# One block for the attention scores of a pair of heads, and unread products behind the last

## The chip, the core and the metric

The kernel runs on one core of one Trainium2 chip. Its engines work side by side, each through its own queue in order: TensorE (PE, with its weight loads as PEld), VectorE (DVE), ScalarE (ACT), GpSimd (POOL) and SyncE (SP, which here issues most of the copies between the chip's memory and the core). TensorE writes only into the eight accumulation banks (PSUM); DVE and ACT read them. The metric is the device time of one execution in microseconds.

## The reference

Two layers of a decoder trunk on 256 tokens of width 1024. The part that the change touches is the differential attention of 8 heads, each with two maps of head dimension 64:

```python
s = jnp.einsum('bqhmd,bkhmd->bhmqk', q_blk, k).astype(jnp.float32) * scale
...
s = jnp.where(mask, s, neg)
p = jax.nn.softmax(s, axis=-1)
a = p[:, :, 0] - lam * p[:, :, 1]
return jnp.einsum('bhqk,bkhe->bqhe', a.astype(v.dtype), v)
```

Around it stand projections, a spatial gating branch, two gated feed-forward networks per layer and layer norms:

```python
for l in range(DEPTH):
    h = _swiglu(x, ffn_w1[l, 0], ffn_w3[l, 0], ffn_w2[l, 0])
    x = _layernorm(ALPHA * x + 0.5 * h, ln_g[l, 0], ln_b[l, 0])
    h = _mixer(x, l, ...)
    x = _layernorm(ALPHA * x + h, ln_g[l, 1], ln_b[l, 1])
    h = _swiglu(x, ffn_w1[l, 1], ffn_w3[l, 1], ffn_w2[l, 1])
    x = _layernorm(ALPHA * x + 0.5 * h, ln_g[l, 2], ln_b[l, 2])
```

## The kernel before

Every large product is computed from operands split into a high and a low part in the type fp32r, which TensorE takes in one pass. The weights come as raw float32 (`raw`, 1 MB per load, four buffers, issued by SP at L153); ACT makes the high part (`whi`, L166) and DVE the low part (`wlo`, L168), each with eight buffers.

Two routines carry most of TensorE's work. `gemm_a2` (L210) takes the weights as the stationary operand. For each block of 128 output rows it issues eight products of 512 columns with the high weights (L220) and later eight products of 256 columns with the low ones (L227); a step for a pair of output blocks is thus 16 products of L220 and 16 of L227. ACT then reads one half of each bank (L228) and DVE adds the other (L230 or L232). `gemm_b` (L249) and `gemm_b2` (L269) take the tokens as the stationary operand, three products of 512 columns per block (L208); the very last call of `gemm_b` cuts its second tile of tokens into two parts of 256 columns, so that the last normalization can begin earlier.

The order of TensorE's instructions is the order in which the program text issues them. Smaller work is threaded in as "tasks": `beside(task, delay)` enters a generator, `beat(w)` moves a clock by the share of main work just issued (0.65 after eight products of L220, 0.35 after eight of L227, n/1024 after a row step of n columns), and a task whose time has come issues its next part at that point, until its next `yield d`, which sets it back by d. On ACT, DVE and POOL a scheduler orders the instructions by priority and by the hints in `behind(...)`.

The eight accumulation banks are four "main" ones for the large products and four "side" ones for everything threaded in. A new side bank waits until the readers of the tile that last had it are done.

The attention of a pair of heads `hp` goes as follows. `rope` projects q, then k, with `gemm_a2`; SP copies the halves of the result crosswise (`swap`, L545), POOL multiplies by the sines (L549), DVE by the cosines (L548), and DVE adds the two a little later (L553). The task `attend`, entered 3.9 after k, then does:

- scores of the second tile of tokens (`exps(1)`, L573): two side banks, one for each of the two maps, and four products of 256 columns, each over 64 partitions (the lower half for map 0, the upper for map 1), in plain float32, which is recorded as two passes a product;
- DVE adds the mask and takes the row maximum (L581), ACT the exponential and its sum (L583);
- 0.6 later the scores of the first tile (`exps(0)`): two more side banks, four products of 128 columns, and the same on DVE and ACT; then the division and the difference of the two maps on DVE (L599, L600, L592);
- 2.6 later six transposes (L607, L612) into two side banks, which ACT copies (L609, L614); 2.3 later the products with the values (L620, L622), read by ACT (L625, L630); then the norm on POOL (L633 and `rsqrt4`) and ACT (L639), transposes back (L644), and the split into `hb` by ACT and DVE (L649, L650).

Four such tasks per layer overlap with each other and with the projections that follow (the gates, `wa`).

Of the kernel before, what the change touches and what calls it, by code (L numbers as in the profile page):

```python
# [19 lines left out]
P = 128  # L20
# [9 lines left out]
HD = 64  # L30
# [20 lines left out]
def trunk(ctx, tc, x, xT, w13a, w13b, w2, wb, wqk, wa, wbr, wo, gateb, sgug, sgub, sguwT, sgubias, lam, diffg,  # L51
          lng, lnb, lngT, lnbT, cosT, sinT, out):
    nc = tc.nc
    V, A, G, PE = nc.vector, nc.scalar, nc.gpsimd, nc.tensor
# [15 lines left out]
    def name(s):  # L70
        serial[0] += 1
        return f"{s}_{serial[0]}"

    def bank():
        return psum.tile([P, 512], F32, tag="main", name=name("bank"))

    def side_bank():
        return psum.tile([P, 512], F32, tag="side", name=name("sbank"))

    def slots(s, n, dtype=F32):  # L80

        return [act.tile([P, 512], dtype, tag="slot", name=name(s)) for _ in range((n + 1) // 2)]
# [8 lines left out]
    def parts(f):  # L91
        return (lambda k: f(k)[:, :T]), (lambda k: f(k)[:, T:])
# [4 lines left out]
    def s512(s, n=4):  # L97
        return tmp.tile([P, 512], F32, tag="side", name=name(s), bufs=n)

    def sm(s, n, dtype=F32, bufs=2):  # L100
        return small.tile([P, n], dtype, tag=f"{s}{n}", name=name(s), bufs=bufs)
# [31 lines left out]
    def beside(task, delay):  # L133
        tasks.append([clock[0] + delay, task])
# [8 lines left out]
    def behind(ins):  # L143

        return tc.issue_after(ins) if ins is not None else nullcontext()
# [93 lines left out]
    def rows_b(ps, t, k0, piece, xh, xl, kts, c0=0, n=512):  # L239

        hi, lo = piece
        for j in range(2):
            k, o = k0 + j, j * 512 + c0
            wh, wl = (w[j][:, c0 : c0 + n] if isinstance(w, list) else w[:, o : o + n] for w in (hi, lo))
            three(ps[:, :n], xh(k)[:, t * P : (t + 1) * P], xl(k)[:, t * P : (t + 1) * P], wh, wl,
                  k == 0, k == kts - 1)
        beat(n / 1024)

    def gemm_b(src, kts, xh, xl, done, tail=4, last=()):  # L249

        blocks = [[(bank(), c, n) for c, n in (last if t else ()) or ((0, 512),)] for t in range(NT)]
        held = []
        for c in range(0, kts, 4):
            nk = min(4, kts - c)
            for i, piece in enumerate(stream(src[:, c * 512 : (c + nk) * 512], nk * 512)):
                k = c + 2 * i
                if k >= kts - tail:
                    held.append((k, piece))
                    continue
                for t in range(NT):  # L260
                    for ps, o, n in blocks[t]:
                        rows_b(ps, t, k, piece, xh, xl, kts, o, n)
        for t in range(NT):
            for ps, o, n in blocks[t]:
                for k, piece in held:
                    rows_b(ps, t, k, piece, xh, xl, kts, o, n)
                done(t, ps[:, :n], o, n)

    def gemm_b2(srcs, xh, xl, done, norm=None):  # L269

# [253 lines left out]
    def mixer(l, i, norm):  # L524
        xh, xl = parts(both)
# [33 lines left out]
        def attend(hp, qT, kT):  # L559
            mx, sums = sm("mx", 8), sm("sums", 8)  # L560
            c4 = sm("c", 4)
            rc = sm("rc", 4)

            def rows(z, m, j, o, n):
                return z[m * HD : (m + 1) * HD, j * T + o : j * T + o + n]

            def exps(t):

                nk = (t + 1) * P
                banks = [side_bank() for _ in range(2)]  # L570
                for j in range(2):
                    for m in range(2):
                        PE.matmul(banks[m][:, j * nk : (j + 1) * nk], rows(qT, m, j, t * P, P), rows(kT, m, j, 0, nk),  # L573
                                  start=True, stop=True)
                pp = []
                for m in range(2):
                    o = m * 4 + t * 2
                    p = s512("pp", 4)[:, : 2 * nk]
                    for j in range(2):
                        s, a = slice(j * nk, (j + 1) * nk), slice(o + j, o + j + 1)  # L580
                        V.tensor_tensor_reduce(out=p[:, s], in0=banks[m][:, s], in1=mask[:, T - nk :], scale=-1.0,  # L581
                                               scalar=BIG, op0=ALU.add, op1=ALU.min, accum_out=mx[:, a])
                        A.activation(p[:, s], p[:, s], AF.Exp, bias=mx[:, a], scale=-1.0, accum_out=sums[:, a])  # L583
                    pp.append(p)
                return pp

            def less(t, pp):

                nk = (t + 1) * P
                for j in range(2):  # L590
                    s = slice(j * nk, (j + 1) * nk)
                    V.scalar_tensor_tensor(out=pp[0][:, s], in0=pp[1][:, s], scalar=c4[:, t * 2 + j : t * 2 + j + 1],  # L592
                                            in1=pp[0][:, s], op0=ALU.mult, op1=ALU.add)
                return pp[0]

            second = exps(1)
            yield 0.6
            first = exps(0)
            V.reciprocal(out=rc, in_=sums[:, 4:])  # L599
            V.scalar_tensor_tensor(out=c4, in0=rc, scalar=neg_lam[l], in1=sums[:, :4], op0=ALU.mult, op1=ALU.mult)  # L600
            second, first = less(1, second), less(0, first)
            yield 2.6
            b = side_bank()
            for j in range(2):
                for c in range(2):
                    o = (j * 2 + c) * P
                    PE.transpose(b[:, o : o + P], second[:, o : o + P], ident)  # L607
            aT1 = slots("aT", 2)[0]
            A.activation(aT1, b, AF.Copy)  # L609
            b = side_bank()  # L610
            for j in range(2):
                PE.transpose(b[:, j * P : (j + 1) * P], first[:, j * P : (j + 1) * P], ident)  # L612
            aT0 = slots("aT", 2)[0][:, :T]
            A.activation(aT0, b[:, :T], AF.Copy)  # L614
            yield 2.3
            b = side_bank()
            for j in range(2):
                h = hp * 2 + j
                v = [val[c][:, h // 4, (h % 4) * P : (h % 4 + 1) * P] for c in range(2)]
                PE.matmul(b[:, j * P : (j + 1) * P], aT0[:, j * P : (j + 1) * P], v[0], start=True, stop=True)  # L620
                for c in range(2):
                    PE.matmul(b[:, T + j * P : T + (j + 1) * P], aT1[:, (j * 2 + c) * P : (j * 2 + c + 1) * P],  # L622
                               v[c], start=c == 0, stop=c == 1)
            on = slots("on", 2)[0]
            A.activation(on, b, AF.Copy)  # L625
            ss, s2 = sm("ss", 4), sm("s2", 4)
            A.activation(s2, sums[:, :4], AF.Square, scale=(2 * HD * EPS) ** 0.5)
            for q in range(4):
                s = slice(q * P, (q + 1) * P)
                A.activation(b[:, s], b[:, s], AF.Square, accum_out=ss[:, q : q + 1])  # L630
            yield 2
            with behind(turned_by[0]):
                G.tensor_tensor(out=ss, in0=s2, in1=ss, op=ALU.add)  # L633
            r = rsqrt4(ss, 1.0 / (2 * HD))
            yield 2
            for q in range(4):
                s = slice(q * P, (q + 1) * P)
                with behind(emptied[0]):
                    A.activation(on[:, s], on[:, s], AF.Copy, scale=r[:, q : q + 1])  # L639
            yield 0.9  # L640
            b = side_bank()
            for j in range(2):
                for t in range(NT):
                    PE.transpose(b[:, j * T + t * P : j * T + (t + 1) * P], on[:, (t * 2 + j) * P : (t * 2 + j + 1) * P],  # L644
                                  ident)
            dl = dgs[:, l : l + 1]
            for j in range(2):
                h, s = hb[hp * 2 + j], slice(j * T, (j + 1) * T)
                A.activation(h[:, :T], b[:, s], AF.Copy, scale=dl)  # L649
                V.scalar_tensor_tensor(out=h[:, T:], in0=b[:, s], scalar=dl, in1=h[:, :T].bitcast(F32),  # L650
                                        op0=ALU.mult, op1=ALU.subtract)

        for hp in range(HEADS // 2):
            qT = rope(wqk[l, hp, 0], HD ** -0.5)
            kT = rope(wqk[l, hp, 1], 1.0, hp == HEADS // 2 - 1)
            beside(attend(hp, qT, kT), 3.9)

        gates = []
        for br, sec in ((0, GA_), (1, GB_)):
# [17 lines left out]
        for t in range(NT):  # L677
            mv = sm("mv", 2)
            V.bn_aggr(out=mv, in_=vst[t])
            r = rsqrt(mv[:, 1:2], EPS)  # L680
# [152 lines left out]
```

## Time and profile before

| | |
|---|---|
| median of 3 runs | 1244.27 us (1244.17 to 1245.04) |
| profiled execution: its own time | 1244.4 us |
| its span, first to last instruction | 1242.7 us |
| mean granted clock of TensorE | 0.998 |
| DMA, mean over the span | 195 GB/s |

In a line of a group, the count of instructions follows the x, then come the total busy time in us, the mean of one in ns, and the idle time of its engine before them with what ended it. In a line of the timeline the start and the length in us come first; instructions of one kind in succession are put together (x8), from the start of the first to the end of the last. Products on TensorE overlap, so the distance between two starts says what a product costs, not its length.

### The profile page before, as it was taken

What the parts mean: (1) busy time and instruction counts of PE and PEld (TensorE: products, weight loads), DVE (VectorE), ACT (ScalarE), POOL (GpSimd) and SP (SyncE); (2) the same over time, 40 slices, a digit from 0 to 9 for tenths busy, and PEclk for the clock granted to TensorE, in tenths of its full rate; (3) what the DMA queues carried; (4) which work ended last, traced back from release to release, by engine and by line L of the source; (5) the groups of instructions that cost most, each with busy time, mean ns of one, the idle gap of its engine ahead of it and who ended that gap; (6) DMA issues with size and microseconds to landing.
All of it is one profiled execution on the core that took longest, in us unless ns stands there. A gap on an engine that the chain in (4) does not pass through costs nothing.

```text
span 1242.7 us, 17850 instructions
## 1 busy us (share of the span) xinstructions
PE 1233.4 (99%) x6695; PEld 1062.5 (86%) x6695; DVE 873.1 (70%) x1533; ACT 755.6 (61%) x1386; POOL 86.7 (7%) x182
## 2 busy tenths in 40 slices
PE   9999999999999999999999999999999999999997
PEld 8888888888888888888888888888888888888886
DVE  6766567876587977665677765679756879766753
ACT  6776446679665566664466664466785554766640
POOL 0100000244100000000000000002440000000000
PEclk9999999999999999999999999999999999999999
DMA  9755545654753645547545546556556456455540
GB/s 351 278 203 186 221 173 190 224 168 162 256 179 142 249 161 200 182 174 254 199 169 189 190 160 247 203 190 200 171 172 231 156 178 229 170 204 204 170 169 35
DMA packets 40679, 241.87 MB, mean 195 GB/s; under 512 B 5344, under 2 KB 6416, under 8 KB 14480
## 3 DMA queue, kind: packets, MB, share of 16 engines
q1 hardware_dynamic: 36624, 228.08, 51.7%
q0 software_dynamic: 3536, 12.13, 2.9%
q8 instruction: 52, 0.85, 0.3%
q10 hardware_dynamic: 432, 0.52, 0.1%
q14 instruction: 35, 0.29, 0.1%
HBM read 235.47 MB, written 1.05 MB: 190 GB/s over the span
## 4 chain that ended last, share of the span: by engine, by line
PE 99%; DVE 0%; DVEq 0%; issue 0%
PE bank L220 38%; PE bank L208 35%; PE bank L227 20%; PE bank L323 2%; PE sbank L573 1%; PE sbank L459 1%; PE sbank L622 1%; PE sbank L703 1%; PE sbank L335 0%; PE sbank L620 0%; PE sbank L644 0%; PE sbank L493 0%; PE sbank L607 0%; PE sbank L612 0%; DVE xtok L432 0%; DVE xtok L438 0%
## 5 line engine op out<-in xcount | busy, mean ns | idle before, releaser
L168 DVE TENSOR_TENSOR wlo<-raw,whi 128x1024 fp32r<-128x1024 f32 (+1 forms) x442 | 489.7, 1126 | 225.1 <-PE bank L227 129.9
L166 ACT ACTIVATE whi<-raw 128x1024 fp32r<-128x1024 f32 (+1 forms) x442 | 425.9, 978 | 278.8 <-PE bank L208 135.2
L220 PE MATMUL bank<-x,whi 128*128 128x512 f32 x1792 | 426.5, 392 | 0.0
L220 PEld LDWEIGHTS bank<-x,whi 128*128 128x128 f32 x1792 | 330.7, 188 | 69.0 <-issue 2.6
L227 PE MATMUL bank<-x,wlo 128*128 128x256 f32 x1792 | 229.9, 284 | 0.0
L227 PEld LDWEIGHTS bank<-x,wlo 128*128 128x128 f32 x1792 | 224.2, 191 | 4.7
L208 PE MATMUL bank<-whi,hhi 128*128 128x512 f32 (+1 forms) x374 | 141.2, 378 | 0.0
L208 PE MATMUL bank<-wlo,hhi 128*128 128x512 f32 (+1 forms) x374 | 141.0, 377 | 0.0
L208 PE MATMUL bank<-whi,hlo 128*128 128x512 f32 (+1 forms) x374 | 140.9, 377 | 0.0
L228 ACT ACTIVATE r<-bank 128x256 f32<-128x256 f32 x256 | 96.5, 380 | 66.2 <-PE bank L227 65.9
L208 PE MATMUL bank<-whi,x 128*128 128x512 f32 x328 | 106.6, 394 | 0.0
L208 PEld LDWEIGHTS bank<-whi,hlo 128*128 128x128 f32 x374 | 70.4, 188 | 13.1
L208 PEld LDWEIGHTS bank<-whi,hhi 128*128 128x128 f32 x374 | 70.4, 188 | 12.7
L208 PEld LDWEIGHTS bank<-wlo,hhi 128*128 128x128 f32 x374 | 70.4, 188 | 12.6
L208 PEld LDWEIGHTS bank<-whi,x 128*128 128x128 f32 x328 | 61.6, 188 | 12.6
L208 PE MATMUL bank<-wlo,x 128*128 128x512 f32 x164 | 64.0, 390 | 0.0
L465 ACT ACTIVATE xf<-sbank,ln_b,ln_g 128x128 f32<-128x128 f32 x80 | 30.1, 457 | 40.1 <-PE sbank L459 40.1
L230 DVE TENSOR_TENSOR silu<-bank,r 128x256 f32<-128x256 f32 x144 | 54.1, 417 | 0.2
L383 POOL DMA_DIRECT2D bc<-in_lng x6 | 3.2, 531 | 726.1 <-DVE bc L382 726.1
L409 DVE SCALAR_TENSOR_TENSOR xtok<-xtok,bank 128x512 f32<-128x512 f32 (+1 forms) x25 | 16.5, 661 | 42.7 <-PE bank L208 42.7
L549 POOL TENSOR_TENSOR swap<-swap,sin_t 128x512 f32<-128x512 f32 x16 | 25.6, 1600 | 240.8 <-DMA swap<-z 236.4
L208 PE MATMUL bank<-lhi,x 128*128 128x512 f32 x120 | 39.8, 395 | 0.0
(174 smaller groups left out, 1246.3 us busy)
## 6 DMA issues: line engine op xcount, KB each, us to landing
raw<-in_w13a SPq DMA_DIRECT2D x72, 1024.0 KB, 4.9
raw<-in_w SPq DMA_DIRECT2D x40, 1024.0 KB, 4.8
raw<-in_wa SPq DMA_DIRECT2D x24, 1024.0 KB, 5.1
raw<-in_wb SPq DMA_DIRECT2D x16, 1024.0 KB, 4.8
raw<-in_wqk SPq DMA_DIRECT2D x16, 1024.0 KB, 5.0
raw<-in_wbr SPq DMA_DIRECT2D x16, 1024.0 KB, 4.9
raw<-in_w13b SPq DMA_DIRECT2D x12, 1024.0 KB, 5.0
raw<-in_wo SPq DMA_DIRECT2D x8, 1024.0 KB, 4.9
```

The costliest lines, as they stand in the source:

```text
L166: A.activation(h, r, AF.Copy)
L168: V.tensor_tensor(out=w, in0=r, in1=h.bitcast(F32), op=ALU.subtract)
L208: PE.matmul(ps, xx, w, start=start and n == 0, stop=stop and n == 2)
L220: PE.matmul(b[-1], hi[:, k * P : (k + 1) * P], xc(k), start=k == 0, stop=False)
L227: PE.matmul(b[n][:, :T], lo[:, k * P : (k + 1) * P], xc(k)[:, :T], start=False, stop=k == KT - 1)
L228: emptied[0] = A.activation(r[:, s], b[n][:, T:], AF.Copy, scale=scale).ins
L230: a = V.tensor_tensor(out=z[:, s], in0=b[n][:, :T], in1=r[:, s], op=ALU.add)
L323: PE.matmul(ps[t][m], x[:, j, o + t * P : o + (t + 1) * P], y, start=k0 + j == 0 and o == 0 and y is hi, stop=k0 + j == KT - 1 and y is lo)
L409: V.scalar_tensor_tensor(out=self.y[t][:, s], in0=self.y[t][:, s], scalar=self.scale, in1=ps, op0=ALU.mult, op1=ALU.add)
L459: PE.transpose(b[:, k * P : (k + 1) * P], self.y[t][:, h * 512 + k * P : h * 512 + (k + 1) * P], ident)
L465: A.activation(xf[:, s], b[:, s], AF.Identity, scale=self.gT[:, f], bias=self.bT[:, f])
L549: turned_by[0] = G.tensor_tensor(out=s3, in0=s3, in1=s, op=ALU.mult).ins
```

## The change

The scores of both tiles of tokens are issued as one block: `scores(1)` and `scores(0)` each take two side banks and issue their products, one after the other, and only then come the mask, maximum and exponentials of both tiles. The `yield 0.6` between them is gone. The task is entered at 4.5 instead of 3.9, the transposes come 2.9 instead of 2.6 after the scores, the products with the values 1.9 instead of 2.3 after the transposes. As the program is built, the merged block stands where the first tile's scores stood (eight products of L220 later than the second tile's did), the transposes stand between the two halves of a run of 16 products of L227 instead of before it, and the rest keeps its place on TensorE. On SP, once per layer, a weight load comes ahead of the copy of the last k's halves instead of behind it. Lines from L573 on are 24 to 27 lines further down in the changed kernel: the scores are at L597, the transposes at L634 and L639.

Behind the last product of the last `gemm_b`, a new function `idle` issues 52 products whose results nobody reads, into two side banks, with the last weights and activations as operands: 10 with 128 columns, then over 64 partitions (alternating halves and banks) 16 with 256 columns and 16 with 128, then 2 with 512 and 8 with 64 columns over all partitions.

```diff
@@ gemm_b
                 done(t, ps[:, :n], o, n)
+        if last:
+            idle(held, xh, xl)
+
+    def idle(held, xh, xl):
+
+        banks = [side_bank() for _ in range(2)]
+        (k, (hi, lo)), (k1, (hi1, lo1)) = held[-2:]
+        ws = [xh(k)[:, :P], xl(k)[:, :P], xh(k1)[:, :P], xl(k1)[:, :P]]
+        ms = [hi[:, :512], lo[:, :512], hi1[:, :512], lo1[:, :512]]
+
+        def one(i, n, m=None):
+            r = slice(0, P) if m is None else slice(m * HD, (m + 1) * HD)
+            PE.matmul(banks[m or 0][:, :n], ws[i % 4][r], ms[i % 4][r, :n], start=True, stop=True)
+
+        for i in range(10):
+            one(i, P)
+        for n in (256, P):
+            for i in range(8):
+                for m in range(2):
+                    one(i, n, m)
+        for i in range(2):
+            one(i, 512)
+        for i in range(8):
+            one(i, 64)
@@ attend
-            def exps(t):
+            def scores(t):
 
                 nk = (t + 1) * P
                 banks = [side_bank() for _ in range(2)]
...
+                return banks
+
+            def exps(t, banks):
+                nk = (t + 1) * P
                 pp = []
...
-            second = exps(1)
-            yield 0.6
-            first = exps(0)
+            banks = [scores(t) for t in (1, 0)]
+            second, first = exps(1, banks[0]), exps(0, banks[1])
             V.reciprocal(out=rc, in_=sums[:, 4:])
...
-            yield 2.6
+            yield 2.9
...
-            yield 2.3
+            yield 1.9
@@ mixer
-            beside(attend(hp, qT, kT), 3.9)
+            beside(attend(hp, qT, kT), 4.5)
```

## The prediction

> **What bounds the kernel now.** I read the page first (busy time by engine), then the list of waits, then the groups by shape, then the timeline of TensorE alone around the attention scores, and last the timeline of the end.
>
> ```profile
> span 1242.7 us, 17850 instructions
> PE 1233.4 (99%) x6695; PEld 1062.5 (86%) x6695; DVE 873.1 (70%) x1533; ACT 755.6 (61%) x1386; POOL 86.7 (7%) x182
> ...
> PE sbank L335 <- DVE warm L331: 1.0, 1, 1.0
> ```
>
> TensorE is busy for 99% of the span, and the only wait put down to it is 1.0 us before the very first product. So time is the sum of the distances between TensorE's products; other engines count only where they make it wait. The distance between products of one kind comes from the last projection, where nothing disturbs them:
>
> ```profile
> 1215.17 0.39 PE L208 MATMUL bank<-whi,hlo 128*128 128x512 f32 x1
> ...
> 1224.02 0.39 PE L208 MATMUL bank<-whi,hlo 128*128 128x512 f32 x1
> 1224.25 0.28 PE L208 MATMUL bank<-whi,hhi 128*128 128x256 f32 x1
> ...
> 1234.20 0.28 PE L208 MATMUL bank<-whi,hlo 128*128 128x256 f32 x1
> ```
>
> From 1215.17 to 1224.02 there are 39 distances: 0.227 us for a product of 512 columns. From 1224.25 to 1234.20 there are 83: 0.120 us for 256 columns. (The duration in a row is longer than the distance, since products overlap.) Whatever a side block takes beyond these distances is its price.
>
> **The change part by part.** *The scores.* These are the products over 64 partitions, each recorded as two passes:
>
> ```profile
> L573 PE MATMUL sbank<-qk,qk 64*128 64x256 f32 x64 | 10.1, 404 | 0.0
> L573 PE MATMUL sbank<-qk,qk 64*128 64x128 f32 x64 | 5.7, 297 | 0.0
> ```
>
> That is 16 blocks of 8 passes: for each of 4 pairs of heads in 2 layers, a block with 256 columns (second tile of tokens) and later one with 128 (first tile). TensorE's timeline of the second pair, whole and in narrow windows:
>
> ```profile
> 248.08 0.28 PE L227 MATMUL bank<-x,wlo 128*128 128x256 f32 x1
> 248.29 1.13 PE L573 MATMUL sbank<-qk,qk 64*128 64x256 f32 x8
> 248.29 0.49 PE L573 MATMUL sbank<-qk,qk 64*128 64x256 f32 x2
> 248.61 0.81 PE L573 MATMUL sbank<-qk,qk 64*128 64x256 f32 x6
> 249.04 0.38 PE L573 MATMUL sbank<-qk,qk 64*128 64x256 f32 x2
> 249.35 0.50 PE L220 MATMUL bank<-x,whi 128*128 128x512 f32 x1
> 251.09 0.40 PE L220 MATMUL bank<-x,whi 128*128 128x512 f32 x1
> 251.42 0.38 PE L573 MATMUL sbank<-qk,qk 64*128 64x128 f32 x2
> 251.63 0.50 PE L573 MATMUL sbank<-qk,qk 64*128 64x128 f32 x6
> 251.75 0.39 PE L573 MATMUL sbank<-qk,qk 64*128 64x128 f32 x4
> 252.06 0.50 PE L220 MATMUL bank<-x,whi 128*128 128x512 f32 x1
> ```
>
> The passes start two at a time, one on each half of the partitions. Inside a block, pairs of passes follow at (249.04 - 248.61) / 2 = 0.215 us with 256 columns and at 0.11 us with 128 (the two last rows of that block end together, so 0.50 - 0.39 lies between their starts). Around this stands the price of going in and out of the 64-partition form:
> - in: the first pass of the 128 block starts 0.33 us after a 512 product that should take 0.23, so 0.10 late; its second pair comes 0.21 after the first where 0.11 is the rule, again 0.10. Together 0.20. The 256 block gives 0.21 - 0.12 = 0.09 and 0.32 - 0.215 = 0.10.
> - out: after the last pair at 249.04 the next main product starts 0.31 later, 0.10 beyond the pair's own 0.215, and that product lasts 0.50 where 0.39 or 0.40 is usual, which delays the next by 0.11. Together 0.21. After the 128 block (last pair at 251.86, one distance of 0.11 behind 251.75): 0.20 - 0.11 = 0.09 and 0.10, so 0.19.
>
> Changed, the 128 passes follow the 256 passes directly. One way out and one way in vanish per pair of heads: 0.20 + 0.20 = 0.40 us; 8 times, 3.2 us. Before shows no 256 pass followed by a 128 pass of this form. Bounds: nothing gained at all if passes into two other banks pay the switch again (0), and 0.50 if the first 128 pair follows a 256 pair at 0.11 instead of 0.215. I take 0.40: inside a block, passes already alternate between two banks with no such loss.
>
> The Trainium skill, "TensorEngine Tiling (Array Packing)", section Key Properties, says that changing the tiling mode drains TensorE, while changing only the tile does not. The rows agree so far: about 0.2 us at each border of a block, none between its halves. By that rule a change of columns and bank is no change of mode and the merged block has one entry and one exit, the same 3.2 us.
>
> *The stall in the last pair.* The 256 block took 1.13 us above, but not in the fourth pair of each layer:
>
> ```profile
> 277.25 2.15 PE L227 MATMUL bank<-x,wlo 128*128 128x256 f32 x16
> 279.33 1.60 PE L573 MATMUL sbank<-qk,qk 64*128 64x256 f32 x8
> ...
> 279.20 0.48 DVE L650 SCALAR_TENSOR_TENSOR hb<-sbank,dgs,hb 128x256 fp32r<-128x256 f32 x1 [0.82 <-ACT hb L649]
> ...
> 894.12 1.65 PE L573 MATMUL sbank<-qk,qk 64*128 64x256 f32 x8
> ```
>
> The list of waits does not name it on TensorE, but the block's first product starts at 279.33 and the rest follow once DVE has read the output of the first pair of heads (L650, ends 279.68), whose side bank the second product needs. Price: 1.60 - 1.13 = 0.47 and 1.65 - 1.13 = 0.52, together 0.99 us. The block now stands behind eight more 512 products, 8 x 0.227 = 1.8 us later, and this read is long done. I count the whole 0.99; bounds 0 (another bank's reader is late in its place, see the rivals) and 0.99.
>
> *What moves with it.* The 256 scores move down past eight L220 products, to where the 128 scores stood. The softmax loses little by that, because DVE was late for it anyway: it took up the second tile's scores only at 283.02, after the first tile's had started at 282.91.
>
> ```profile
> 282.91 0.71 PE L573 MATMUL sbank<-qk,qk 64*128 64x128 f32 x8
> ...
> 283.02 0.41 DVE L581 CUSTOM_DVE_ANT_0 pp<-sbank,mask 128x256 f32<-128x256 f32 x1
> ```
>
> Without that cover a late softmax would make the transposes (L607, L612) wait. But they also move down, behind eight more L227 products (8 x 0.120 = 0.96 us). Their own switch between eight L227 and eight L227 products instead of L220 and L227 I cost at nothing, with 0.1 us either way per pair as bound. The products with the values (L620, L622), the norm and the transposes back (L644) keep their places among the main products.
>
> On SP's queue, in each layer, the last copy of halves (swap) is now issued after a weight load instead of before it:
>
> ```profile
> raw<-in_wa SPq DMA_DIRECT2D x24, 1024.0 KB, 5.1
> swap<-z SPq DMA_DIRECT2D x64, 64.0 KB, 2.2
> 272.38 0.69 DVE L553 TENSOR_TENSOR qk<-qk,swap 128x512 f32<-128x512 f32 x1 [1.28 <-POOL swap L549]
> ```
>
> At worst it lands with that load, 5.1 - 2.2 = 2.9 us later. Queued behind it: POOL's product with the sines, DVE's sum L553, and on DVE whatever follows. That sum ran at 272.38, the scores that need it came at 279.33 and come later now, so 2.9 us are covered by about 7; without the cover they would stand in front of the fourth score block. Price 0.
>
> *The unread products.* 52 products follow the last one that counts: 10 with 128 columns, 16 with 256 and 16 with 128 over 64 partitions, 2 with 512, 8 with 64. Nobody reads them, but the program's end waits for TensorE. Their cover is the last normalization and the last output copy:
>
> ```profile
> 1238.78 1.12 SPq L440 DMA_DIRECT2D out_x<-xtok  x2
> out_x<-xtok SPq DMA_DIRECT2D x2, 128.0 KB, 2.0
> ```
>
> The second of these copies is issued in the last 0.33 us before 1239.90, about 1239.57, and lands 2.0 later, 1241.6. TensorE is free from 1234.20 + 0.12 = 1234.3. Cover: 7.3 us. The trace has no product of these operands (fp32r, one pass) under 256 columns and none over 64 partitions. Nearest for a narrow one is the distance in the products with the values:
>
> ```profile
> 255.19 0.61 PE L622 MATMUL sbank<-val,aT 128*128 128x128 f32 x4
> 255.64 0.39 PE L620 MATMUL sbank<-val,aT 128*128 128x128 f32 x2
> ```
>
> 0.45 / 4 = 0.11 us a pass. In pairs like the scores: 10 x 0.11 + 8 x 0.12 + 8 x 0.11 + 2 x 0.23 + 8 x 0.11 + 0.4 for in and out = 4.7 us. Without pairing 16 x 0.12 + 16 x 0.11 replace the middle: 6.5 us. With two passes for all but the two of 512, in pairs: 10 x 0.22 + 8 x 0.43 (twice 0.215) + 8 x 0.22 + 0.46 + 8 x 0.22 + 0.4 = 10.0. Two passes and no pairing: 2.2 + 16 x 0.24 + 16 x 0.22 + 0.46 + 1.76 + 0.4 = 12.2. I take 4.7, hidden: every recorded fp32r product is one record, and the form over 64 partitions does start in pairs. The ends are 0 and 12.2 - 7.3 = 4.9.
>
> **Sum.** -3.2 - 0.99 + 0 = -4.2 us. The profiled execution took 1244.4 us (span 1242.7 and 1.7 around it); 1244.4 - 4.2 = 1240.2. The median of the runs shown is 1244.27, 0.1 lower, so 1240.1.
>
> **The rivals.**
> A, *a wait for the fourth bank.* A block now needs all four side banks, so in pairs two to four it also waits for ScalarE's copies of the previous pair's transposed weights:
>
> ```profile
> L166 ACT ACTIVATE whi<-raw 128x1024 fp32r<-128x1024 f32 (+1 forms) x442 | 425.9, 978 | 278.8 <-PE bank L208 135.2
> ...
> 277.11 0.38 PE L612 MATMUL sbank<-ident,pp 128*128 128x128 f32 x2
> ...
> 280.01 0.58 ACT L609 ACTIVATE aT<-sbank 128x512 f32<-128x512 f32 x1
> 280.49 0.38 ACT L614 ACTIVATE aT<-sbank 128x256 f32<-128x256 f32 x1
> ```
>
> For: the copy ended at 280.59, 3.1 us after the transposes; only 0.96 + 1.82 + about 0.1 = 2.9 us of products now lie between. Against: as the changed program is built, one weight conversion fewer stands before it on ScalarE (L166, 0.98 us) and one short read-out of a bank more, which leaves some 0.5 us of slack. If one conversion slips back in front, the fourth block waits about 0.6 in each layer: 1240.1 + 1.2 = 1241.3; if all six blocks wait 0.6, 1243.7.
>
> B, *the unread products outlast the end.* One mechanism: the narrow single-pass products run as two passes, one after the other. Then 4.9 us stick out: 1240.1 + 4.9 = 1245.0, slower than before. It decides from a mean of (7.3 + 4.2) / 52 = 0.22 us a product. For: no such product is in the trace. Against: the single records, and fp32 passes of this width take 0.11. With pairing, 10.0 - 7.3 = 2.7 stick out: 1242.8.
>
> C, *the change does not merge anything.* The passes into the other two banks pay out and in again. Then only the stall goes: 1244.3 - 1.0 = 1243.3. Against: passes alternate between banks today without it.
>
> **How the numbers follow.** Forecast 0.62 (1240.1), A 0.15 (1241.3; half of it under 1241.8), B one after the other 0.10 (1245.0), B in pairs 0.07 (1242.8), C 0.05 (1243.3), and 0.01 for a softmax so late that transposes wait by more than everything gained. A measurement of this kernel can tell about 0.2%, 2.5 us, from no change: faster is under 1241.8, slower over 1246.8. Faster: 0.62 + 0.08 from A = 0.70. Slower: half of B's first case, 0.05, because no row bounds a narrow product from above, and the softmax, 0.06 in all. The same: the other halves of A and B, 0.07 + 0.05, B in pairs and C, 0.24. Range: down to 0.50 a pair, 1240.1 - 0.8 = 1239.3; up to B in pairs and most of A, 1242.8, which leaves out a little under 2 in 10.
>
> **What would show it.** Right: per pair of heads one run of 16 passes on L597, first half 0.215 and second 0.11 apart, with one late main product after it instead of two; 256 passes of the fourth pairs as quick as the others; TensorE's last unread product before the last output copy lands; no new wait of TensorE. Wrong: a gap inside the 16 passes after the second, third or fifth product (A, if a copy on ScalarE ends just before it) or between the 256 and the 128 half (C); an end of the span that follows TensorE's last product instead of the copy (B); transposes that start late after DVE's L620.

## The result, and the profile after

| | before | changed |
|---|---|---|
| median | 1244.13 us (1243.49 to 1245.04, 8 runs) | 1240.67 us (1240.34 to 1241.41, 8 runs) |
| the same kernels once more, beside a later experiment | 1244.26 us (1243.78 to 1244.84, 13 runs) | 1241.37 us (1240.15 to 1242.34, 8 runs) |
| profiled execution: its own time, its span | 1244.4, 1242.7 us | 1241.04, 1239.3 us |

The ratio is 0.9974 with a 95% interval of 0.9964 to 0.9983, and 0.9976 (0.9965 to 0.9986) the second time. The change makes the kernel faster by about 3 us; the two medians lie 0.6 and 1.3 us above the 1240.1 that was forecast. First the page of the changed kernel, its span and busy times:

```profile
span 1239.3 us, 17964 instructions
## 1 busy us (share of the span) xinstructions
PE 1234.4 (100%) x6747; PEld 1067.3 (86%) x6747; DVE 874.2 (71%) x1533; ACT 754.7 (61%) x1386; POOL 90.3 (7%) x182
```

TensorE has 52 instructions more, the unread ones, and is still what the span consists of. The list of TensorE's waits (line, releaser: us in total, times, longest):

```profile
PE sbank L359 <- DVE warm L355: 1.0, 1, 1.0
PE sbank L597 <- ACT aT L636: 0.2, 1, 0.2
```

The first row was there before. The second is new: the scores (L597) wait once for ScalarE's copy of the transposed weights (L636), which is rival A. First the ordinary case, TensorE's timeline of the second pair, whole and in narrow windows:

```profile
249.61 0.39 PE L220 MATMUL bank<-x,whi 128*128 128x512 f32 x1
249.93 1.58 PE L597 MATMUL sbank<-qk,qk 64*128 64x256 f32 x16
250.68 0.83 PE L597 MATMUL sbank<-qk,qk 64*128 64x256 f32 x10
250.89 0.61 PE L597 MATMUL sbank<-qk,qk 64*128 64x128 f32 x8
251.00 0.50 PE L597 MATMUL sbank<-qk,qk 64*128 64x128 f32 x6
251.44 0.96 PE L220 MATMUL bank<-x,whi 128*128 128x512 f32 x3
251.77 0.39 PE L220 MATMUL bank<-x,whi 128*128 128x512 f32 x1
```

All 16 passes stand in one run, and the 128 half follows the last pair of the 256 half at 250.89 - 250.68 = 0.21 us, as one 256 pair follows another; the next 128 pair comes 0.11 later. There is no border between the halves. From here on the *price* of a block is the time from the start of the last main product before it to the start of the second main product after it, less what these two main products usually take (0.228 us for 512 columns, 0.120 for 256, the distances of the prediction to a thousandth): 251.77 - 249.61 - 2 x 0.228 = 1.70 us, at more digits 1.706. In the kernel before the block of 256 cost 1.266 and that of 128 0.849, together 2.115. The gain is 0.41 us a pair.

Then the fourth pair of each layer, on TensorE:

```profile
276.99 0.38 PE L639 MATMUL sbank<-ident,pp 128*128 128x128 f32 x2
...
280.09 1.58 PE L597 MATMUL sbank<-qk,qk 64*128 64x256 f32 x16
...
889.62 0.38 PE L639 MATMUL sbank<-ident,pp 128*128 128x128 f32 x2
...
892.71 0.70 PE L597 MATMUL sbank<-qk,qk 64*128 64x256 f32 x2
893.61 1.57 PE L597 MATMUL sbank<-qk,qk 64*128 64x256 f32 x14 [0.20 <-ACT aT L636]
```

and on ScalarE:

```profile
276.67 0.91 ACT L693 ACTIVATE gate<-gz,gbh 128x256 f32<-128x256 f32 x2
277.48 0.45 ACT L676 ACTIVATE hb<-sbank,dgs 128x256 fp32r<-128x256 f32 x1
277.83 1.05 ACT L166 ACTIVATE whi<-raw 128x1024 fp32r<-128x1024 f32 x1
278.78 0.46 ACT L676 ACTIVATE hb<-sbank,dgs 128x256 fp32r<-128x256 f32 x1
279.14 0.38 ACT L228 ACTIVATE r<-bank 128x256 f32<-128x256 f32 x1
279.40 0.60 ACT L636 ACTIVATE aT<-sbank 128x512 f32<-128x512 f32 x1
...
890.22 0.91 ACT L693 ACTIVATE gate<-gz,gbh 128x256 f32<-128x256 f32 x2 [0.28 <-DVE gz L230]
...
892.96 0.60 ACT L636 ACTIVATE aT<-sbank 128x512 f32<-128x512 f32 x1
```

In layer 1 the copy ends at 280.00, and the block, whose second product takes the bank that the copy reads, starts at 280.09 and runs through: a margin of 0.1 us. In layer 2 the copy ends at 893.56; the first product's two passes are out at 892.71, the other 14 follow only at 893.61. They would have started with the first, so the wait is 893.61 - 892.71 = 0.90, of which the list names 0.2. The price of that block is 2.595 instead of 1.706.

Another reader ends at the very same time: DVE's read for `hb`, the one that stalled the kernel before (L650 there, L677 here).

```profile
893.08 0.47 DVE L677 SCALAR_TENSOR_TENSOR hb<-sbank,dgs,hb 128x256 fp32r<-128x256 f32 x1
```

It ends at 893.55, too. Which of the two TensorE waited for shows in the distance from the reader's end to TensorE's start. Over all ten waits in the profiles of merged blocks below, it is 0.05 us behind the copy each time, but anything from 0.02 to 0.08 us behind L677. In the kernel before, where L650 was waited for, it was 0.15. So the wait is for the copy. The old read has not become early, though: it ends 0.1 us before the block starts in layer 1 and 0.8 behind its start in layer 2, and only does no harm because the block's second product no longer takes its bank.

The eight merged blocks cost 7 x 1.706 + 2.595 = 14.5 us; the sixteen of before cost 17.9 (twelve ordinary ones and the second halves of the fourth pairs at 1.266 and 0.849, and the two first halves that stalled, 1.730 and 1.787). That is 3.4 us, as much as 1242.7 - 1239.3. The agreement is in part luck: TensorE is 0.2 us later in the changed kernel's profile before any of the change is reached, and 0.2 were won outside these blocks.

The end, on TensorE and SP:

```profile
1230.83 0.28 PE L208 MATMUL bank<-whi,hlo 128*128 128x256 f32 x1
1230.95 0.22 PE L280 MATMUL sbank<-whi,hhi 128*128 128x128 f32 x1
...
1232.45 0.28 PE L280 MATMUL sbank<-whi,hhi 64*128 64x256 f32 x2
1232.57 0.28 PE L280 MATMUL sbank<-wlo,hlo 64*128 64x256 f32 x2
...
1235.25 0.28 PE L280 MATMUL sbank<-whi,hhi 128*128 128x64 f32 x1
1235.36 0.28 PE L280 MATMUL sbank<-wlo,hlo 128*128 128x64 f32 x1
...
1235.41 1.12 SPq L464 DMA_DIRECT2D out_x<-xtok  x2
```

Each unread product is one record, those over 64 partitions start two at a time (x2) 0.12 apart, and the last ends at 1235.64: 4.7 us after 1230.95. The last output copy is issued only about then (1235.41, and the second of the two some 0.8 later).

### The profile page after: what moved, and what is told of

Read it like the earlier page. It is cut to its first block, busy times and chain, and to the rows that moved or that the text cites. A ratio compares the mean times of both kernels' runs of the same rounds, so it can differ in the third digit from the quotient of the medians.

```text
span 1239.3 us, 17964 instructions
## 1 busy us (share of the span) xinstructions
PE 1234.4 (100%) x6747; PEld 1067.3 (86%) x6747; DVE 874.2 (71%) x1533; ACT 754.7 (61%) x1386; POOL 90.3 (7%) x182
## 3 DMA queue, kind: packets, MB, share of 16 engines
HBM read 235.47 MB, written 1.05 MB: 191 GB/s over the span
## 4 chain that ended last, share of the span: by engine, by line
PE 97%; ACT 1%; DVE 1%; issue 0%; DMA 0%; SPq 0%; POOL 0%; DVEq 0%; POOLq 0%
PE bank L220 37%; PE bank L208 35%; PE bank L227 19%; PE bank L347 2%; PE sbank L597 1%; PE sbank L483 1%; PE sbank L730 1%; PE sbank L649 1%; ACT pp L611 0%; PE sbank L359 0%; PE sbank L517 0%; PE sbank L647 0%; PE sbank L671 0%; PE sbank L634 0%; DMA swap<-z 0%
## 5 line engine op out<-in xcount | busy, mean ns | idle before, releaser
L220 PE MATMUL bank<-x,whi 128*128 128x512 f32 x1792 | 425.4, 391 | 0.0
L220 PEld LDWEIGHTS bank<-x,whi 128*128 128x128 f32 x1792 | 330.8, 188 | 66.2
L227 PE MATMUL bank<-x,wlo 128*128 128x256 f32 x1792 | 231.2, 284 | 0.0
L227 PEld LDWEIGHTS bank<-x,wlo 128*128 128x128 f32 x1792 | 225.2, 191 | 5.4
L228 ACT ACTIVATE r<-bank 128x256 f32<-128x256 f32 x256 | 96.8, 379 | 64.6 <-PE bank L227 64.1
L573 POOL TENSOR_TENSOR swap<-swap,sin_t 128x512 f32<-128x512 f32 x16 | 28.5, 1780 | 242.4 <-DMA swap<-z 141.9
```

Source lines behind the costliest of these rows:

```text
L220: PE.matmul(b[-1], hi[:, k * P : (k + 1) * P], xc(k), start=k == 0, stop=False)
L227: PE.matmul(b[n][:, :T], lo[:, k * P : (k + 1) * P], xc(k)[:, :T], start=False, stop=k == KT - 1)
L228: emptied[0] = A.activation(r[:, s], b[n][:, T:], AF.Copy, scale=scale).ins
L573: turned_by[0] = G.tensor_tensor(out=s3, in0=s3, in1=s, op=ALU.mult).ins
```

## The experiments

Prices below are worked out as above; "first three pairs" stands for those of both layers, and they agree within 0.002 us. Spans are those of the profiled execution. They also hold a scatter that no edit here touches: TensorE's 100th product of the large kind starts between 27.8 and 28.8 us after the span's start in these eleven profiles (before 28.4, changed 28.6).

| run | median us | ratio (95%) | span | price, first three pairs | price, fourth pairs |
|---|---|---|---|---|---|
| before | 1244.13 | 1 | 1242.7 | 1.266 + 0.849 | 1.730 and 1.787, + 0.85 |
| changed | 1240.67 | 0.9974 (0.9964 to 0.9983) | 1239.3 | 1.706 | 1.705, 2.595 |
| merged, no unread products | 1240.89 | 0.9972 (0.9962 to 0.9983) | 1239.5 | 1.706 | 2.038, 2.233 |
| unread products alone | 1244.36 | 1.0002 (0.9993 to 1.0011) | 1243.5 | 1.27 + 0.85 | 1.719 and 2.246, + 0.85 |
| form broken in the block | 1244.35 | 1.0001 (0.9993 to 1.001) | 1242.1 | 2.170 | 2.412, 2.536 |
| unread products twice | 1242.91 | 0.999 (0.9981 to 0.9999) | 1240.4 | 1.705 | 1.705, 2.452 |
| moved, not merged | 1242.59 | 0.9988 (0.9979 to 0.9996) | 1240.9 | 1.263 + 0.839 | 1.263 + 0.838 |
| merged at the old place | 1243.12 | 0.9991 (0.9982 to 1.0) | 1241.9 | 1.708 | 3.326, 3.368 |
| fourth pair later | 1240.60 | 0.9969 (0.9957 to 0.9981) | 1239.1 | 1.705 | 1.700, 1.700 |
| both waits covered | 1240.49 | 0.9972 (0.9961 to 0.9983) | 1238.3 | 1.706 | 1.700, 1.701 |
| changed, once more | 1241.37 | 0.9976 (0.9965 to 0.9986) | 1239.7 | 1.706 | 2.750, 2.564 |

**Each half of the change alone.** The merged scores without the unread products:

```diff
@@ gemm_b
-        if last:
-            idle(held, xh, xl)
```

> The changed kernel without its 52 unread products. If the gain is all in the attention and the unread products lie beside the last normalization and the last copy, the time is that of the changed kernel, 1240.7 us, and the eight blocks of 16 passes keep their price of 1.71 us beyond the main products' own distances. Rival: the unread products take part in the gain or hide a cost; then the time leaves 1240.7 by more than half a us. The wait in the fourth block of the second layer (0.89 us in the profile) may come and go between executions.

1240.89 us: all of the gain. Here the fourth pairs wait in both layers, by 2.038 - 1.706 = 0.33 and by 0.53 us. The other half is the kernel before with `idle` and its call:

```diff
@@ gemm_b (before)
+        if last:
+            idle(held, xh, xl)
```

> The kernel before with the 52 unread products behind its last one and nothing else. They take 4.7 us and have 7.3 us of cover, so the time is that of before, 1244.1 us. Rival: something else that the longer tail brings (a later end of TensorE, more instructions to fetch) moves the time by more than half a us either way.

1244.36 us, no change that can be told. The unread products cost nothing, and they bring nothing. The stall of the fourth pairs in the kernel before is itself no constant: 1.719 and 2.246 here against 1.730 and 1.787 in the first profile.

**Is it the border of the form?** A transpose over all 128 partitions between the halves brings back one way out and one way in, with nothing moved. What it writes is overwritten by the scores.

```diff
@@ scores
+                if t == 0:
+                    PE.transpose(banks[0][:, :P], ident, ident)
```

> The changed kernel with one unread 128-column transpose over all partitions between the 256-column and the 128-column scores of every pair, so that TensorE leaves the 64-partition form and comes back inside the block, at the same place among the main products. If the borders of the form are the price (0.20 out and 0.20 in), each of the eight blocks grows by 0.11 for the transpose and 0.40 for the two borders, 8 x 0.51 = 4.1 us: about 1244.8. Rival: what was gained is that one group of main products fewer is interrupted, whatever the form; then only the transposes are paid, 8 x 0.11 = 0.9 us: 1241.6.

1244.35 us, as slow as before. TensorE's timeline of the second pair of this run:

```profile
249.66 1.13 PE L599 MATMUL sbank<-qk,qk 64*128 64x256 f32 x8
250.73 0.33 PE L596 MATMUL sbank<-ident 128*128 128x128 f32 x1
250.99 0.71 PE L599 MATMUL sbank<-qk,qk 64*128 64x128 f32 x8
```

The block costs 2.170 instead of 1.706: 0.464 more, of which 0.11 is the transpose itself and 0.355 the two borders. So the price lies in leaving and entering the form over 64 partitions and not in the number of blocks; the expected 0.51 was somewhat high. Eight times 0.464 is 3.7 us, and the medians lie 1244.35 - 1240.67 = 3.7 apart. The spans lie only 2.8 apart: this execution was 0.7 us earlier at the 100th large product, and its fourth pairs waited 0.3 us less.

**How far does the cover of the unread products reach?**

```diff
@@ gemm_b
             idle(held, xh, xl)
+            idle(held, xh, xl)
```

> The changed kernel with the 52 unread products issued twice, which leaves TensorE busy for another 4.7 us. In the changed kernel's profile its last unread product ends at 1235.64 and the last output copy, issued at about 1236.2, lands about 2.0 later, at 1238.2: 2.6 us of cover are left. So 4.7 - 2.6 = 2.1 us should stick out: 1242.8. Rival: the end does not wait for TensorE's products; then 1240.7.

1242.91 us, the 1242.8 expected. The last rows of this run's timeline on TensorE and SP:

```profile
1239.21 0.28 PE L281 MATMUL sbank<-wlo,hlo 128*128 128x64 f32 x1
...
1234.64 1.12 SPq L465 DMA_DIRECT2D out_x<-xtok  x2
```

The last copy is issued at about 1235.4 and lands 2.0 later, 1237.4; TensorE ends at 1239.49 and the span at 1240.4. Here TensorE sets the end, 2.1 us behind the copy's landing as expected; in the changed kernel the copy does.

**Moving and merging apart.** The kernel before, with each of its two blocks where the changed kernel's delays put it, but still two blocks:

```diff
@@ attend, mixer (before)
-            yield 2.6
+            yield 2.3
...
-            yield 2.3
+            yield 1.9
...
-            beside(attend(hp, qT, kT), 3.9)
+            beside(attend(hp, qT, kT), 4.5)
```

> The kernel before with the changed kernel's delays but two blocks of scores, 0.6 apart as before: the 256-column scores stand where the merged block stands, the 128-column ones eight main products later. No unread products. If merging and moving are two separate terms, the blocks keep their prices of before (1.27 and 0.85 us, 2.12 a pair) and only the wait in the fourth pairs (0.47 and 0.52 us) goes: about 1243.1. Rival: the place brings the gain; then 1240.7.

1242.59 us. The fourth pair of layer 1 on this run's timeline:

```profile
280.68 1.13 PE L573 MATMUL sbank<-qk,qk 64*128 64x256 f32 x8
```

The stall of the fourth pairs is gone in both layers, without merging. All score blocks together cost 16.8 us, 1.1 less than before; the span is 1.8 shorter. Of the other 0.7, 0.3 lie in the first 28 us of the span, ahead of the change; where the rest lies was not followed. The reverse, the merged block at the old place:

```diff
@@ attend, mixer
-            yield 2.9
+            yield 3.2
...
-            yield 1.9
+            yield 2.3
...
-            beside(attend(hp, qT, kT), 4.5)
+            beside(attend(hp, qT, kT), 3.9)
```

> The merged block entered at 3.9 as before, 1.8 us earlier than in the changed kernel, transposes and products with the values where they were before (3.2 and 2.3). If merging alone is worth 0.41 us a pair, blocks that do not wait cost 1.71 as well; but with four banks taken at the earlier place, the fourth pairs wait for the copies and for the read that already held them up before: between 0.5 and 2.5 us a layer, so 1241 to 1245. Rival: the banks are free in time there as well; then 1239.8.

1243.12 us. Its fourth pair of layer 1, on TensorE and ScalarE:

```profile
278.44 0.70 PE L597 MATMUL sbank<-qk,qk 64*128 64x256 f32 x2
280.06 1.57 PE L597 MATMUL sbank<-qk,qk 64*128 64x256 f32 x14 [0.93 <-ACT aT L636]
...
279.41 0.60 ACT L636 ACTIVATE aT<-sbank 128x512 f32<-128x512 f32 x1
```

The copy ends at 280.01, the 14 passes start at 280.06, 1.62 us after the first. Merging gains the same 0.41 a pair, 3.3 us in all, but the two fourth pairs now wait 3.3 us, where the kernel before lost 0.99 to its stalls: 1.0 us of the gain is left in the blocks. The merge needs the later place; the two parts of the change aren't independent gains.

**Can the remaining wait go?** The fourth pair's scores later by one more step:

```diff
@@ mixer
-            beside(attend(hp, qT, kT), 4.5)
+            beside(attend(hp, qT, kT), 5.1 if hp == HEADS // 2 - 1 else 4.5)
```

> The changed kernel with the fourth pair's block another eight main products later (entered at 5.1 instead of 4.5). If the wait of 0.89 us in the second layer's fourth block is for ScalarE's copies of the third pair's transposes, the copies are now 1.8 us ahead and all eight blocks cost 1.71: 0.9 us less than the changed kernel in its profile, about 1239.8. Rival: pushing the fourth pair later brings a new wait behind it (its transposes, its products with the values or the end of the mixer), and nothing or less than nothing is won.

1240.60 us, not 1239.8. The wait for the copies did go; another came. The second pair's transposes back in layer 1, and the scaling (`on`) that they read, in the changed kernel:

```profile
288.63 0.60 PE L671 MATMUL sbank<-ident,on 128*128 128x128 f32 x4
...
286.11 1.27 ACT L666 ACTIVATE on<-on,nwy 128x128 f32<-128x128 f32 x4
```

and in this run, with the conversion that stands ahead on ScalarE:

```profile
288.54 0.85 PE L671 MATMUL sbank<-ident,on 128*128 128x128 f32 x4
...
283.02 1.04 ACT L166 ACTIVATE whi<-raw 128x1024 fp32r<-128x1024 f32 x1
...
287.74 1.27 ACT L666 ACTIVATE on<-on,nwy 128x128 f32<-128x128 f32 x4
```

The scaling, in the changed kernel done 1.25 us before the transposes begin, now ends at 289.01, after their start at 288.54. With the fourth pair's exponentials due later, one more conversion goes ahead of them on ScalarE, and they still stand ahead of the scaling. That is about half of the 1.6 us by which the scaling is late; the other half is the lateness of the whole row of work on ScalarE in this execution (its copy L636 starts at 280.19 instead of 279.40). Either alone would have fitted into the 1.25 us. These blocks cost 0.691 and 0.953 in the two layers instead of 0.444, so 0.76 of the 0.89 came back. So these transposes were moved too, by eight products of L220:

```diff
@@ attend, beside the edit above
-            yield 0.9
+            yield 1.55 if hp == 1 else 0.9
```

> As e6 (the fourth pair's scores later in each layer), and the second pair's transposes back (L671) stand eight products of L220 (1.8 us) later. In e6 these transposes began before ScalarE had finished scaling `on` (L666) and took 0.25 us longer in one layer and 0.51 in the other. Theory: TensorE has no other bound than its own order and the two readers on ScalarE, so with both covered the 0.76 us go: 0.8 below e6, 1239.8, the second pair's transposes back cost their usual 0.44, the score blocks 1.70. Rival: each move pushes a further reader late, and the time stays with e6 at 1240.6, with a wait of 0.3 or more in another side block.

> The changed kernel once more, on the same chip as the run before: 1240.7 by both theories, with 0.5 to 0.9 us of wait in the fourth pairs' score blocks.

In its profile no wait is left but that before the very first product, every block costs its least (the transposes back 0.44), and the span is the shortest of all:

```profile
290.35 0.60 PE L671 MATMUL sbank<-ident,on 128*128 128x128 f32 x4
...
287.26 1.27 ACT L666 ACTIVATE on<-on,nwy 128x128 f32<-128x128 f32 x4
```

The times say it less clearly: 1240.49 us (1239.68 to 1242.79, 6 runs) against 1241.37 (1240.15 to 1242.34) for the changed kernel on the same chip, and 1239.8 was expected. It is faster than the kernel before; that it is faster than the changed one is not shown, since the two intervals against before overlap almost wholly. One execution took 1242.79, and there is no profile of it. The changed kernel's second profile has the wait in both layers; layer 1:

```profile
279.42 0.70 PE L597 MATMUL sbank<-qk,qk 64*128 64x256 f32 x2
280.47 1.57 PE L597 MATMUL sbank<-qk,qk 64*128 64x256 f32 x14 [0.35 <-ACT aT L636]
...
279.82 0.60 ACT L636 ACTIVATE aT<-sbank 128x512 f32<-128x512 f32 x1
```

280.47 - 279.42 = 1.05 us where the first profile of the same kernel has none, and 0.86 in layer 2: together 1.9.

## Why the prediction came out as it did

**The merge: right.** 0.40 us a pair was forecast from the borders of the old blocks, 0.41 was measured, 3.3 us in all. The run with the form broken shows that it is these borders, and the rows show none between the halves, so rival C (nothing merges) falls.

**The stall in the last pair: cause right, size wrong.** That the stall goes with the place is shown by the blocks moved without being merged. But "I count the whole 0.99" held only if no other reader came late, and two steps behind it failed: the slack of the copy, "some 0.5 us", and the copy of halves on SP's queue, "Price 0". The net of this term is 0.99 - 0.89 = 0.1 us in the first profile of the changed kernel and 0.99 - 1.9 = -0.9 in the second. Forecast -3.2 - 0.99 = -4.2, measured in the first profile -3.3 - 0.1 = -3.4.

*The slack* was counted from two different marks. The 3.1 us to the copy's end run from the end of the last transposes (277.49), the 2.9 us of products from the start of the product behind them (277.25). From 277.25 the copy ended 3.3 us later. Less 0.98 for the conversion and plus 0.26 to 0.38 for the read-out (distance and length of L228 in the rows above) that is 2.6 to 2.7, so 0.1 to 0.3 us of slack were left and not 0.5.

*What stands ahead of the copy* on ScalarE was counted right: between the last transposes and the copy lie two `hb`, one conversion and one read-out `r`, one conversion fewer than before and one read-out more. From the start of `gate` to the start of the copy this row of work takes 279.40 - 276.67 = 2.73 us in layer 1 and 892.96 - 890.22 = 2.74 in layer 2. But its start lies 0.32 before the transposes at 276.99 in layer 1 and 0.60 behind those at 889.62 in layer 2, and those 0.9 us are the wait. TensorE's second score product is due 280.09 - 276.99 = 3.1 us after the transposes, and the copy ended 3.0 after them in one layer and 3.9 in the other. In the kernel before it ended 3.48 and 3.54 after them, so its two layers gave no warning.

*What starts the row* is the copy of halves. Layer 2 of the kernel before:

```profile
879.50 2.53 SPq L545 DMA_DIRECT2D swap<-z  x4
883.86 0.33 SPq L153 DMA_DIRECT2D raw<-in_wa  x1
...
887.22 0.69 DVE L553 TENSOR_TENSOR qk<-qk,swap 128x512 f32<-128x512 f32 x1 [1.28 <-POOL swap L549]
```

and of the changed one:

```profile
875.65 2.17 SPq L153 DMA_DIRECT2D raw<-in_wa  x2
879.67 2.42 SPq L569 DMA_DIRECT2D swap<-z  x4
...
886.74 1.29 POOL L573 TENSOR_TENSOR swap<-swap,sin_t 128x512 f32<-128x512 f32 x1 [2.13 <-DMA swap<-z]
889.04 0.68 DVE L577 TENSOR_TENSOR qk<-qk,swap 128x512 f32<-128x512 f32 x1
```

Issued behind the weight load, these four copies took 5.1 to 6.4 us to land instead of 2.2 to 3.4; the load landed at 885.95 and the last of them at 886.58. POOL waits for them, DVE's sum comes after POOL, `gz` after the sum, `gate` after `gz`. The sum starts 0.6 us before the last transposes (889.62), where it started 4.7 before them in the kernel before (887.22, transposes at 891.90). From the landing of the last copy of halves to the end of L636 it is 7.0 us in both layers of both profiles of the changed kernel. It is 7.0 in ten of the twelve layers of all profiles with the merged block at this place or the fourth pair later (without the inserted transpose), 7.1 and 7.5 in the other two, and 11.9 in the kernel before, where this chain held nothing up. In the changed kernel's two profiles the landing lies 4.0, 3.0, 2.9 and 3.1 us before the transposes, and the waits are 0, 0.89, 1.04 and 0.86: each is what the landing falls short of 3.9. So the prediction was right that the load could push these copies back (by 2.9 us at worst, it said; against the transposes it was 4.4 to 5.5), but it looked only at the scores, which need the sum late. It priced "whatever follows" on DVE at nothing, and through `gz` and `gate` that leads to the read that frees the bank. No run puts the copies back ahead of the load in the merged kernel, so that this alone would end the wait is not shown.

**Rival A: half right, and it should have had more weight.** Its place (the fourth pair of each layer) and its row (L636) are what the profiles show; it was priced at 0.6 a layer, 1.2 in all. The gap inside the 16 passes comes after the first product, where it was looked for after the second, third or fifth. And what makes the copy late is not an additional conversion in front of it, as the rival had it, but the late start of the row. Four profiles of the merged block at this place (the changed kernel twice, without the unread products, with twice as many) show 0.89, 1.9, 0.86 and 0.75 in all: 1.1 in the mean. The forecast's own case, no wait at all, is in none of them. The rival's 1241.3 is nearer to the second median, 1241.37, and the forecast 1240.1 nearer to the first, 1240.67. The other pairs never waited.

**The unread products: right.** 4.7 us forecast, 4.7 measured, single passes and in pairs, hidden behind the last normalization and the last copy. Alone they change nothing, and doubled they end the span. Rival B falls in both forms.

**What was costed at nothing: right but for the copy of halves.** The transposes at their new place cost 0.656 a pair, against 0.655 to 0.661 before. No transpose waited for a softmax, and the first score passes of the fourth pairs start at their usual 0.32 after the main product, so k itself was there in time although its last halves were issued behind a weight load. What else waited for these halves is told above.

## What to carry to other kernels

Where products over part of the partitions stand between full ones, count the borders: here each way in and each way out cost about 0.2 us, and blocks of the same form put together save it. A block that takes more buffers at once waits for more readers, so its place has to be chosen for the slowest of them; at the old place the same merge lost most of what it gained. Before a slack is counted on, count both of its ends from the same mark, and follow back what starts the engine that has to keep it. A small copy that falls behind a big load on its queue is covered only if everything that waits for it is, down to the last read that frees a buffer.

## What the runs showed of the hardware that was not expected

Two things. A product of fp32r with 64 columns, each with weights of its own, costs no less than one with 128: the last eight unread products follow each other at 0.11 us (1235.25 and 1235.36 above), as the ten with 128 columns do. And a form broken by a single transpose costs less than a block's full way out and in: 0.355 us beside the transpose's own 0.11, where two separate blocks pay 0.41 more than a merged one.
